# Binary cross-entropy on one core: the second half's negation moved behind the next chunk's clips

## The chip, the core and the metric

The kernel runs on one core of a Trainium2 chip. The metric is the device time of one execution in microseconds (us), as the median of several runs; lower is better. The engines that matter here are VectorE (DVE in the profile), ScalarE (ACT), GpSimd (POOL), whose instruction queue issues nearly all DMAs, and the core's 16 DMA engines, which move data between the chip's memory (HBM) and the on-chip buffer (SBUF).

## What is computed

```python
pred   = uniform(0.01, 0.99, (8192, 8192))  # float32
target = randint(0, 2, (8192, 8192))        # float32, 0 or 1
def reference(pred, target):
    eps = 1e-7
    pred = np.clip(pred, eps, 1 - eps)
    return -(target * np.log(pred) + (1 - target) * np.log(1 - pred))
```

Each of the three arrays holds 67,108,864 float32 values (268 MB). Since target is 0 or 1, one of the two terms is always zero, and the kernel uses that: the result is -log(|pred + target - 1|).

## The kernel before

The arrays are taken as one flat row of values and cut into chunks. A chunk is 128 partitions by some width: first one of 8192 columns (chunk 0), then 35 of 14336 columns (chunks 1 to 35; the name `z` is 35), then a tail of 6656, 6656 and 1024 columns (chunks 36 to 38, named a, b, c). Two buffers stay in SBUF. `ring_p` holds three wide chunks of pred in float32; a chunk is worked on in place there and stored from there. `ring_t` has room for one wide chunk of target, which the load turns into bfloat16 on the way.

The work on a chunk, in two halves of its columns (`halves`), is:

- `clip` (line 85, VectorE, tensor_scalar with max and min) bounds pred;
- `merge` (line 91, VectorE, scalar_tensor_tensor) makes pred + (target - 1); ScalarE then takes the absolute value (line 94) and the logarithm (line 95);
- `negate` (line 99, VectorE, tensor_scalar times -1) gives the result.

The DMAs of a wide chunk are `load_p` (line 70, pred), `load_t` (line 73, target) and `store` (line 79). All three are issued from GpSimd's queue (only chunk 0's pred comes through ScalarE's queue, and the tail's stores through SyncE's).

The order is written out by hand (`tc.manual_schedule()`): each engine takes its instructions in the order in which the program names them, and waits at an instruction until what it needs is there. One turn of the loop over k (lines 110 to 120) gives VectorE two merges of chunk k, the two negations of chunk k, and the two clips of chunk k+1. It gives ScalarE absolute value and logarithm of each half of chunk k. It gives GpSimd's queue the load of target k+1 (which waits for both merges, since `ring_t` holds one chunk only), the store of chunk k (which waits for the second negation) and the load of pred k+2 (which overwrites the slot of chunk k-1). Lines 121 to 141 finish chunk 35 and the tail.

Of the kernel before, what the change touches and what calls it, by code (L numbers as in the profile page):

```python
# [1 line left out]

# [4 lines left out]

EPS = 1e-7

WIDE = 14336  # L10
SLOTS = 3
TAIL = (6656, 6656, 1024)
ROWS = (108, 12, 8)


@with_exitstack
def kernel(
    ctx: ExitStack,
    tc: tile.TileContext,
    pred: bass.AP,  # L20
    target: bass.AP,
    out: bass.AP,
):
    nc = tc.nc
    fp32 = mybir.dt.float32
    low = mybir.dt.bfloat16
    Alu = mybir.AluOpType
    Act = mybir.ActivationFunctionType
    P = nc.NUM_PARTITIONS

    R, C = pred.shape
    total = R * C // P
    rest = total - sum(TAIL)
    n = rest // WIDE
    first = rest - n * WIDE
    assert 0 < first <= WIDE and n > 4 and sum(TAIL) <= WIDE
    spots = [(first, 0)]
    spots += [(WIDE, k % SLOTS * WIDE) for k in range(1, n + 1)]
    c = (n + 1) % SLOTS * WIDE
    for w in TAIL:  # L40
        spots.append((w, c))
        c += w
    n = len(spots)
    z = n - 1 - len(TAIL)
    starts = [sum(w for w, _ in spots[:k]) * P for k in range(n)]

    pool = ctx.enter_context(tc.tile_pool(name="rings", bufs=1))
    ring_p = pool.tile([P, SLOTS * WIDE], fp32, name="ring_p", tag="ring_p")
    ring_t = pool.tile([P, WIDE], low, name="ring_t", tag="ring_t")
    warm = pool.tile([1, 8], fp32, name="warm", tag="warm")  # L50

    def chunk(ap, k):
        flat = ap.rearrange("r c -> (r c)")
        w = spots[k][0]
        return flat[starts[k] : starts[k] + w * P].rearrange("(p w) -> p w", p=P)

    def cols(ring, k, part, c):
        w = spots[k][0]
        i, m = part
        return ring[:, c + i * w // m : c + (i + 1) * w // m]  # L60

    def p_of(k, part=(0, 1)):
        return cols(ring_p, k, part, spots[k][1])

    def t_of(k, part=(0, 1)):
        return cols(ring_t, k, part, spots[k][1] % WIDE)

    def load_p(k):
        queue = nc.scalar if k == 0 else nc.gpsimd
        queue.dma_start(out=p_of(k), in_=chunk(pred, k))  # L70

    def load_t(k):
        nc.gpsimd.dma_start(out=t_of(k), in_=chunk(target, k))  # L73

    def store(k):
        queue = nc.sync if k > z else nc.gpsimd
        r = 0
        for rows in ROWS if k == n - 1 else (P,):
            queue.dma_start(out=chunk(out, k)[r : r + rows, :], in_=p_of(k)[r : r + rows, :])  # L79
            r += rows  # L80
        assert r == P

    def clip(k, *part):
        p = p_of(k, *part)
        nc.vector.tensor_scalar(  # L85
            out=p, in0=p, scalar1=EPS, scalar2=1 - EPS, op0=Alu.max, op1=Alu.min
        )

    def merge(k, *part):
        p, t = p_of(k, *part), t_of(k, *part)  # L90
        nc.vector.scalar_tensor_tensor(  # L91
            out=p, in0=t, scalar=1.0, in1=p, op0=Alu.subtract, op1=Alu.add
        )
        nc.scalar.activation(out=p, in_=p, func=Act.Abs)  # L94
        nc.scalar.activation(out=p, in_=p, func=Act.Ln)  # L95

    def negate(k, *part):
        p = p_of(k, *part)
        nc.vector.tensor_scalar(out=p, in0=p, scalar1=-1.0, scalar2=None, op0=Alu.mult)  # L99

    halves = (0, 2), (1, 2)
    with tc.manual_schedule():
        load_p(0)
        load_t(0)
        load_p(1)
        nc.vector.memset(warm, 1.0)  # L106
        nc.scalar.activation(out=warm, in_=warm, func=Act.Ln)  # L107
        for h in halves:
            clip(0, h)
        for k in range(z):  # L110
            for h in halves:
                merge(k, h)
            load_t(k + 1)
            for h in halves:
                negate(k, h)
            for h in halves:
                clip(k + 1, h)
            store(k)
            if k + 2 <= z:
                load_p(k + 2)  # L120
        for h in halves:
            merge(z, h)
        a, b, c = range(z + 1, n)
        for j in a, b, c:
            load_p(j)
            load_t(j)
        negate(z, halves[0])
        clip(a)
        negate(z, halves[1])
        store(z)  # L130
        merge(a)
        clip(b)
        merge(b)
        negate(a)
        store(a)
        clip(c)
        merge(c)
        negate(b)
        store(b)
        negate(c)  # L140
        store(c)


# [1 line left out]
_INS = ['pred', 'target']  # L145
_OUTS = [((8192, 8192), 'float32')]


# [23 lines left out]
```

## Time and profile before

| what | value |
|---|---|
| median of three runs | 1867.55 us (1865.96 to 1867.95) |
| the profiled execution itself | 1868.84 us |
| its span, first to last instruction | 1867.1 us |
| VectorE busy | 1118.2 us, 60% of the span |
| ScalarE busy | 901.7 us, 48% |
| GpSimd busy | 283.3 us, 15% |
| moved by the 16 DMA engines | 671.14 MB, mean 359 GB/s |
| HBM read and written | 536.87 MB and 268.44 MB, 431 GB/s over the span |
| one merge of 128x7168 | about 7.6 us |
| one clip or negation of 128x7168 | about 3.9 us |
| one absolute value or logarithm of 128x7168 | about 6.2 us |

The profile is of one execution. Busy shares are averages over the span. In a line of the timeline, the first number is the start in microseconds from the span's beginning, the second the busy time, then come engine, source line, operation, output and input; the brackets say how long the engine sat idle before it and what released it. In a table by windows the last two columns are the mean busy share of the 16 DMA engines and the rate that they moved. The rate counts target once it is bfloat16, so the load of target shows half the rate of the other transfers at the same speed of reading. A "time to landing" runs from the issue of a DMA to the moment at which all of its data are there, the time that it stands in line behind others included.

### The profile page before, as it was taken

What the parts mean: (1) busy time and instruction counts of PE and PEld (TensorE: products, weight loads), DVE (VectorE), ACT (ScalarE), POOL (GpSimd) and SP (SyncE); (2) the same over time, 40 slices, a digit from 0 to 9 for tenths busy, and PEclk for the clock granted to TensorE, in tenths of its full rate; (3) what the DMA queues carried; (4) which work ended last, traced back from release to release, by engine and by line L of the source; (5) the groups of instructions that cost most, each with busy time, mean ns of one, the idle gap of its engine ahead of it and who ended that gap; (6) DMA issues with size and microseconds to landing.
All of it is one profiled execution on the core that took longest, in us unless ns stands there. A gap on an engine that the chain in (4) does not pass through costs nothing.

```text
span 1867.1 us, 695 instructions
## 1 busy us (share of the span) xinstructions
DVE 1118.2 (60%) x226; ACT 901.7 (48%) x152; POOL 283.3 (15%) x117
## 2 busy tenths in 40 slices
DVE  4675665655556555665665556655566665556664
ACT  3555444444555555444444555555544444455555
POOL 0121111111111101111111111101111111111100
DMA  9999999999999999999999999999999999999998
GB/s 331 336 373 373 364 355 359 356 355 355 354 354 359 373 373 373 370 356 362 356 354 358 354 354 356 367 373 373 373 362 360 359 354 359 354 354 354 360 366 346
DMA packets 16869, 671.14 MB, mean 359 GB/s; under 512 B 1888, under 2 KB 1888, under 8 KB 2272
## 3 DMA queue, kind: packets, MB, share of 16 engines
q0 software_dynamic: 16272, 659.56, 98.5%
q1 hardware_dynamic: 448, 7.34, 0.9%
q10 hardware_dynamic: 144, 4.19, 0.6%
q14 instruction: 5, 0.04, 0.0%
HBM read 536.87 MB, written 268.44 MB: 431 GB/s over the span
## 4 chain that ended last, share of the span: by engine, by line
DMA 67%; issue 28%; DVE 2%; ACT 2%; POOL 0%; POOLq 0%; DVEq 0%; PEldq 0%
DMA ring_t<-in_target_dram 67%; DVE ring_p L91 2%; ACT ring_p L95 1%; ACT ring_p L94 1%; DVE ring_p L99 0%; POOL out_dram L79 0%; POOL ring_p L70 0%; DVEq L167 0%; POOLq L73 0%; POOLq L79 0%; DVEq L91 0%; PEldq L167 0%
## 5 line engine op out<-in xcount | busy, mean ns | idle before, releaser
L94 ACT ACTIVATE ring_p<-ring_p 128x7168 f32<-128x7168 f32 (+3 forms) x75 | 451.6, 6021 | 943.5 <-DVE ring_p L91 943.5
L91 DVE SCALAR_TENSOR_TENSOR ring_p<-ring_t,ring_p 128x7168 f32<-128x7168 bf16 (+3 forms) x75 | 554.8, 7436 | 236.9 <-DMA ring_t<-in_target_dram 236.8
L99 DVE TENSOR_SCALAR ring_p<-ring_p 128x7168 f32<-128x7168 f32 (+3 forms) x75 | 285.0, 3801 | 475.0 <-ACT ring_p L95 475.0
L95 ACT ACTIVATE ring_p<-ring_p 128x7168 f32<-128x7168 f32 (+3 forms) x75 | 452.1, 6028 | 2.4
L85 DVE TENSOR_SCALAR ring_p<-ring_p 128x7168 f32<-128x7168 f32 (+3 forms) x75 | 281.8, 3798 | 20.1 <-DMA ring_p<-in_pred_dram 20.1
L79 POOL DMA_DIRECT2D out_dram<-ring_p x36 | 127.4, 3540 | 730.3 <-DVE ring_p L99 730.3
L73 POOL DMA_DIRECT2D ring_t<-in_target_dram x39 | 20.7, 532 | 802.9 <-DVE ring_p L91 802.1
L70 POOL DMA_DIRECT2D ring_p<-in_pred_dram x38 | 135.3, 3560 | 0.0
L107 ACT ACT_TABLE_LOAD x1 | 1.3, 1283 | 1.1 <-PEq L156 1.1
L106 DVE MEMSET warm<- 1x8 f32 x1 | 0.1, 65 | 0.8 <-PEq L156 0.8
L107 ACT ACTIVATE warm<-warm 1x8 f32<-1x8 f32 x1 | 0.2, 208 | 0.0
L156 POOL MEMSET const-float32-0.0<- 128x1 f32 x1 | 0.1, 98 | 0.2 <-issue 0.2
L156 POOL MEMSET const-bfloat16-1.0<- 128x1 bf16 x1 | 0.1, 101 | 0.0
L156 POOL MEMSET const-float32-1.0<- 128x1 f32 x1 | 0.1, 98 | 0.0
L156 POOL MEMSET const-uint8-127<- 128x1 uint8 x1 | 0.1, 98 | 0.0
## 6 DMA issues: line engine op xcount, KB each, us to landing
ring_p<-in_pred_dram POOLq DMA_DIRECT2D x35, 7168.0 KB, 44.3
out_dram<-ring_p POOLq DMA_DIRECT2D x35, 7168.0 KB, 31.0
ring_t<-in_target_dram POOLq DMA_DIRECT2D x35, 3584.0 KB, 35.2
ring_p<-in_pred_dram POOLq DMA_DIRECT2D x2, 3328.0 KB, 33.6
out_dram<-ring_p SPq DMA_DIRECT2D x2, 3328.0 KB, 15.1
ring_p<-in_pred_dram ACTq DMA_DIRECT2D x1, 4096.0 KB, 19.5
out_dram<-ring_p POOLq DMA_DIRECT2D x1, 4096.0 KB, 21.4
ring_t<-in_target_dram POOLq DMA_DIRECT2D x2, 1664.0 KB, 28.8
```

The source lines that it names most:

```text
L70: queue.dma_start(out=p_of(k), in_=chunk(pred, k))
L73: nc.gpsimd.dma_start(out=t_of(k), in_=chunk(target, k))
L79: queue.dma_start(out=chunk(out, k)[r : r + rows, :], in_=p_of(k)[r : r + rows, :])
L85: nc.vector.tensor_scalar(out=p, in0=p, scalar1=EPS, scalar2=1 - EPS, op0=Alu.max, op1=Alu.min)
L91: nc.vector.scalar_tensor_tensor(out=p, in0=t, scalar=1.0, in1=p, op0=Alu.subtract, op1=Alu.add)
L94: nc.scalar.activation(out=p, in_=p, func=Act.Abs)
L95: nc.scalar.activation(out=p, in_=p, func=Act.Ln)
L99: nc.vector.tensor_scalar(out=p, in0=p, scalar1=-1.0, scalar2=None, op0=Alu.mult)
L106: nc.vector.memset(warm, 1.0)
L107: nc.scalar.activation(out=warm, in_=warm, func=Act.Ln)
L156: nc = _bacc.Bacc("TRN2", target_bir_lowering=False, num_devices=1)
```

## The change

From the third chunk on (k of 2 and more, 33 of the 35 turns of the loop) VectorE's order within a turn is: negate the first half of chunk k, clip both halves of chunk k+1, negate the second half of chunk k. Before, both negations stood ahead of the clips. For k of 0 and 1 the order stays. The store of chunk k and the load of pred k+2 are named behind the last negation, as before. No instruction is added or taken away.

```diff
             for h in halves:
                 merge(k, h)
             load_t(k + 1)
-            for h in halves:
-                negate(k, h)
+            negate(k, halves[0])
+            if k < 2:
+                negate(k, halves[1])
             for h in halves:
                 clip(k + 1, h)
+            if k >= 2:
+                negate(k, halves[1])
             store(k)
             if k + 2 <= z:
                 load_p(k + 2)
```

## The prediction

> **What bounds the kernel now.** I first read the page's row of DMA shares and its queue table.
>
> ```profile
> DMA  9999999999999999999999999999999999999998
> q0 software_dynamic: 16272, 659.56, 98.5%
> q1 hardware_dynamic: 448, 7.34, 0.9%
> q10 hardware_dynamic: 144, 4.19, 0.6%
> ```
>
> The shares of the three queues add up to 100% of 16 engines' span: the DMA engines are hardly ever without a packet, while VectorE is busy for 60% and ScalarE for 48%. Next, the chain that ended last; one turn of its steady pattern is
>
> ```profile
> 713.58 15.49 issue
> ...
> 729.08 35.17 DMA ring_t<-in_target_dram
> ```
>
> Taken alone this looks like a loop: target lands, VectorE merges for 15.2 us, the next target load is issued, and it takes 35.2 us. But those 35.2 us are not a target transfer. The table by windows cuts that turn (713.60 to 764.34 us, 50.74 us long) into thirds:
>
> ```profile
> 713.60:730.51 16.91, 15.16 (x2) 9.19 (x2) 0.53 (x1) 1.00 1.00 434
> 730.51:747.42 16.91, 5.33 (x2) 15.41 (x3) 0.00 (x0) 1.00 1.00 373
> 747.42:764.34 16.92, 10.07 (x3) 0.00 (x0) 7.44 (x2) 1.00 1.01 278
> ```
>
> The last two columns are DMA share and GB/s. The share is 1.00 in each third. A turn moves three equal portions (store, pred, target) of 128x14336 values, in the order of their issue, each in a third, 16.9 us. The target load, issued at 729.08, stands behind what is left of store and pred for some 18 us. So the turn is 3 x 16.9 = 50.7 us of transfer, and the merges hide beside it. The kernel is bound by DMA, and an edit counts only if it leaves DMA engines empty or saves a transfer. This one saves none.
>
> **The change, step by step.** It adds and removes no instruction. In 33 turns it moves one negation (3.89 us) behind two clips (3.81 us from start to start, 7.70 us for the pair). What hangs on it is the order of events in a turn, shown by the timeline:
>
> ```profile
> 729.08 0.53 POOL L73 DMA_DIRECT2D ring_t<-in_target_dram  x1 [22.18 <-DVE ring_p L91]
> 733.71 3.89 DVE L99 TENSOR_SCALAR ring_p<-ring_p 128x7168 f32<-128x7168 f32 x1 [4.92 <-ACT ring_p L95]
> 745.98 3.89 DVE L99 TENSOR_SCALAR ring_p<-ring_p 128x7168 f32<-128x7168 f32 x1 [8.38 <-ACT ring_p L95]
> 749.79 7.70 DVE L85 TENSOR_SCALAR ring_p<-ring_p 128x7168 f32<-128x7168 f32 x2
> 750.17 3.63 POOL L79 DMA_DIRECT2D out_dram<-ring_p  x1 [20.55 <-DVE ring_p L99]
> 753.79 3.82 POOL L70 DMA_DIRECT2D ring_p<-in_pred_dram  x1
> 764.35 15.16 DVE L91 SCALAR_TENSOR_TENSOR ring_p<-ring_t,ring_p 128x7168 f32<-128x7168 bf16 x2 [6.86 <-DMA ring_t<-in_target_dram]
> ```
>
> 1. The gap that the clips would fill. VectorE idles 8.38 us, from 737.60 to 745.98, for ScalarE's second logarithm. The clips need the next pred chunk, issued at 703.09 in the turn before; the look at that one line says when it is there:
>
> ```profile
> L70 POOL DMA_DIRECT2D ring_p<-in_pred_dram x1: 3820/3820/3820, 703.1 to 703.1; - x1
> ...
> DMA to landing us min/median/max: 44.3/44.3/44.3
> ```
>
> 703.1 + 44.3 = 747.4 us. So the clips can't start at 737.6; VectorE now waits there about 9.8 us for pred, past the end of the logarithm at 745.95.
>
> 2. The negation behind them. Clips from 747.4 to 755.1, the negation to 759.0. Queued behind the waiting clips on VectorE are this negation and then the next merges. The merges wait for target, which lands at 764.26, so VectorE still has 5.3 us to spare (it had 6.86 idle, as the clips ended at 757.5). The next turn's merges, target load and logarithms keep their times: cost nothing, hidden by the target transfer; if pred landed 5.3 us later relative to target, it would start to cost.
>
> 3. The store and the pred load behind it on GpSimd's queue. The store is released 0.30 us after the negation's end (749.87 to 750.17 before), so at 759.3 instead of 750.2: 9.1 us later. Beside the clips the two issues took 3.63 and 3.82 us; without VectorE beside it an issue takes 0.53 (the target's line above). VectorE is now idle there, so store and pred are issued by 759.8 and 760.4, against 753.8 and 757.6: only 6.0 and 2.8 us later. The Trainium skill states this for the issues, in "SBUF — State Buffer", section "SBUF: two separate sides": while VectorE runs a fast-mode operation on SBUF, GpSimd can't write DMA descriptors and DMA engines may starve. The trace agrees on 3.63 against 0.53 us; by that rule alone some starvation would end and the kernel gain, by the DMA share of 1.00 none was there to end.
>
> 4. Is 759.8 soon enough? The store follows target on the DMA engines:
>
> ```profile
> 755.88:757.99 2.11, 1.61 (x1) 0.00 (x0) 1.73 (x1) 1.00 1.01 217
> 757.99:760.11 2.12, 0.00 (x0) 0.00 (x0) 0.00 (x0) 1.00 1.01 325
> 760.11:762.22 2.11, 0.00 (x0) 0.00 (x0) 0.00 (x0) 1.00 1.01 380
> 762.22:764.34 2.12, 0.00 (x0) 0.00 (x0) 0.00 (x0) 1.00 1.00 433
> ```
>
> At 217 GB/s all engines carry target, at 433 all carry the store. The hand-over is spread: by the trace's records of single packets (8 per engine and transfer, 2.1 us each) the first engine is through with target at 759.8, the last at 763.9. What is not in the trace is the time from a GpSimd issue to the first packet when the engines have nothing else queued. Nearest rows: pred of chunk 0, issued from ScalarE's queue at 0.73, has its first packet at 1.74, so 1.0 us; the tail's store from SyncE's queue follows its negation (end 1850.4) at 1851.3, 0.9 us. Above, target of chunk 0, issued by GpSimd at 1.23, has its first packet at 6.05, 4.8 us, but behind pred's packets. I take 1.0, as nearest: an idle queue. Then the store can start at 759.3 + 1.0 = 760.3 (760.8 counted from the end of the issue). Engines through at 759.8 wait up to 1 us, once; the last, at 763.9, waits for nothing, with 3.1 to 3.6 us to spare. As target lands only when the last engine is done, the turn stays 50.74 us. Engines that had run ahead are held back, and lose a lead that never counted. With the low end (0 us) nothing waits at all. With 4.8 us the store starts at 764.1, the last engine waits about 0.15 us per turn, 33 x 0.15 = 5 us. The Trainium skill, in "DMA: Bandwidth & Descriptors", section "Latency and other measured facts", gives about 1 us to the first byte for DMAs issued by GpSimd, more than for the other queues; no row here isolates it, and by it the sum would be the same.
>
> 5. The ends. Turns 0 and 1 are as before. In turn 34 the store goes from 1765.5 to about 1774.6, and pred of chunk a just behind it, while target of chunk 35 is in transfer until 1779; the tail isn't touched.
>
> **Sum:** 0 us on the profiled execution's 1868.84 us (span 1867.1 plus 1.7 around it). That run lies 1.3 us above the median of 1867.55, so I give 1867.6 for the median.
>
> **Rivals.**
>
> *The DMA engines fall into step* (slower). The early turns are longer than the late ones: in the chain, target issues lie 51.2 to 51.4 us apart between 168 and 323 us, mostly 50.7 after 470. In the packet records the last target packet of some engines, ahead of the store, takes up to 0.76 us longer while the engines are close in step (ends 0.6 to 3 us apart) and almost never once they are 4.2 us apart. The change holds back the leaders to about 3 us ahead of the last engine. If the engines stay close in step and the last one pays 0.5 us in each of 33 turns, that is 16.5 us, less the 4 us or so that before pays anyway: +12, 1880 us. It decides from the point at which the held-back engines lengthen the last engine's packets, not just their own. Against it: the last engine hands over 3 us after the bunch, alone, and with such a spread the turn from 322 to 373 us took 50.8 us. Chance 0.13.
>
> *The store's first packet comes late* (slower). If it takes more than 4.6 us from issue, every turn waits: at 4.8 us 1872; each further 0.1 us costs 3.3 us. No row asks for more. Chance 0.06.
>
> *The lengthened packets vanish* (faster). At the hand-over at 100 us, where the store was issued only 6 us ahead (94.14), no packet was lengthened, though engines were 0.5 us apart; in others it had been issued 10 us ahead. If a late store spares them, the last engine wins back the 4 us or so by which it falls behind the first: 1863.5, just over 0.2%. Chance 0.06, as it has one hand-over for it.
>
> *The change reaches its gap, but it doesn't matter*: were pred there at 737.6, the store would keep its time, and again nothing would change. It belongs to the forecast's time.
>
> **How the numbers follow.** Forecast, no change: 0.75. The bound for "same" is 0.2%, 3.7 us, about what a measurement of this kernel can tell from no change. Slower: 0.13 + 0.06 = 0.19; faster 0.06; same 0.75. The range goes from 1863 (the rival below) to 1878: it holds the 4.8 us bound (1872) and most of the way to 1880.
>
> **What would show it.** Right: clips (line 85) wait about 9.8 us per turn for pred, some 320 us in all; the second negation waits for nothing; store issues take 0.53 us; time to landing falls from 31.0 to about 22 us for the store (781.2 - 759.3) and from 44.3 to about 38 for pred; turns stay 50.7 us; DMA share 1.00. Wrong: turns above 51 us past 500 us; a DMA share under 0.98 where target ends; target landing before its merges can start, which would put VectorE on the path.

## The result, and the profile after

The changed kernel takes 1880.94 us (median of 4 runs, 1879.8 to 1881.97) against 1866.88 us for the kernel before, measured anew beside it: a ratio of 1.0075, 95% interval 1.0058 to 1.0092. The forecast of no change was wrong, and the range, up to 1878, missed it by 3 us. The profiled execution took 1879.8 us with a span of 1878.0, 10.9 us more than before.

Nearly everything that the prediction said about VectorE and GpSimd is in the profile. From the groups of instructions (line, engine, operation, forms, count, busy us, mean ns, idle us before them and its releaser):

```profile
L85 DVE TENSOR_SCALAR ring_p<-ring_p 128x7168 f32<-128x7168 f32 (+3 forms) x75 | 281.8, 3797 | 344.7 <-DMA ring_p<-in_pred_dram 344.7
...
L99 DVE TENSOR_SCALAR ring_p<-ring_p 128x7168 f32<-128x7168 f32 (+3 forms) x75 | 284.7, 3798 | 198.4 <-ACT ring_p L95 198.4
L79 POOL DMA_DIRECT2D out_dram<-ring_p x36 | 25.5, 708 | 1029.1 <-DVE ring_p L99 1029.1
```

The clips now wait 344.7 us for pred (20.1 before), the negations 198.4 us for the logarithm (475.0 before), and a store issue takes 0.7 us on average (3.5 before). From the table of DMA issues (KB each, median us to landing):

```profile
ring_p<-in_pred_dram POOLq DMA_DIRECT2D x35, 7168.0 KB, 38.7
out_dram<-ring_p POOLq DMA_DIRECT2D x35, 7168.0 KB, 22.3
ring_t<-in_target_dram POOLq DMA_DIRECT2D x35, 3584.0 KB, 35.5
```

The prediction gave about 38 for pred and 22 for the store. The one surprise is target: 35.5 us, where the same table of the kernel before has 35.2. The chain that ended last shows the same as turns, from one target issue to the next. First the kernel before, then the changed one:

```profile
1084.23 35.14 DMA ring_t<-in_target_dram
...
1134.92 35.18 DMA ring_t<-in_target_dram
...
1185.65 35.20 DMA ring_t<-in_target_dram
...
1236.40 35.19 DMA ring_t<-in_target_dram
```

```profile
1087.85 35.31 DMA ring_t<-in_target_dram
...
1138.70 36.23 DMA ring_t<-in_target_dram
...
1190.48 35.42 DMA ring_t<-in_target_dram
...
1241.45 36.16 DMA ring_t<-in_target_dram
```

The turns of the changed kernel are 50.85, 51.78 and 50.97 us long, where before they were 50.69, 50.73 and 50.75. The row of DMA shares and the queue table do not show where that goes:

```profile
DMA  9999999999999999999999999999999999999998
...
q0 software_dynamic: 16272, 659.56, 98.6%
```

The engines count as busy as ever, and the bytes are the same. What fell is the rate, from 359 to 357 GB/s over the whole span. The table by windows of 380 and 400 us (last columns DMA share, GB/s), first of the kernel before, then of the changed one:

```profile
120.00:500.00 380.00, 225.49 (x46) 185.82 (x31) 59.23 (x22) 1.00 1.00 359
900.00:1300.00 400.00, 242.69 (x48) 192.76 (x32) 63.71 (x24) 1.00 1.00 363
```

```profile
120.00:500.00 380.00, 225.97 (x46) 185.76 (x31) 11.07 (x21) 1.00 1.00 359
900.00:1300.00 400.00, 242.74 (x48) 186.78 (x31) 12.66 (x24) 1.00 1.00 357
```

In the first 500 us the two are alike; later the changed kernel moves 357 GB/s instead of 363 at the same share. The size of that step is not to be relied on, since a window cuts turns in two and target counts half: from 1300 to 1700 us the kernel before shows 360 as well. But the turns are longer, and packets in them take longer. One such place, in windows of 2.1 us at the end of a store:

```profile
1131.80:1133.90 2.10, 2.10 (x1) 2.10 (x1) 0.00 (x0) 1.00 1.01 437
1133.90:1136.00 2.10, 2.10 (x1) 2.10 (x1) 0.00 (x0) 1.00 1.33 437
1136.00:1138.10 2.10, 2.10 (x1) 2.07 (x2) 0.00 (x0) 1.00 1.01 437
```

A packet is counted in the window in which it starts, with its whole length. A share of 1.33 says that the packets which start there last a third longer than the others. The trace's records of single packets (8 per engine and transfer, usually 2.12 us each) name no engine; the packets of one engine are found by joining the end of each to the start of the next. By them, these are the last packets of the store: 13 of the 16 engines take 0.7 to 1.1 us longer for them. The other three run over elsewhere, at the end of target. In the next turn, for example, target's last packet takes them 3.15 to 3.24 us instead of 2.13, starting at 1170.3 to 1171.5 us, while the 13 begin the store.

From the store of chunk 1 to that of chunk 34, each of the 13 engines runs over by 9.5 to 11.4 us in all at the store's last packet and by at most 1.1 us at target's last two. With the three it is the other way round: 13.1 to 14.0 us at target's last two packets, at most 0.4 us at the store's last. From turn 14 on it is always these three that are through with target last. Target has landed only when the last engine is through with it, so it is their part that lengthens the turns. In the three turns above the last engine's target packets run over by 0.14, 1.19 and 0.18 us. Over the whole stretch the packets of the engine that is last in most turns run over by 14.7 us, and those of the last engine before by 4.4 us (3.0 at target's end, nearly all in turns 2 to 7). The difference is 10.3 of the 10.9 us by which the span grew.

### The profile page after: what moved, and what is told of

It reads as the page before. It is cut to its first block, busy times and chain, and to the rows that moved or that the text cites. A ratio compares the mean times of both kernels' runs of the same rounds, so it can differ in the third digit from the quotient of the medians.

```text
span 1878.0 us, 695 instructions
## 1 busy us (share of the span) xinstructions
DVE 1117.9 (60%) x226; ACT 901.7 (48%) x152; POOL 72.7 (4%) x117
## 4 chain that ended last, share of the span: by engine, by line
DMA 67%; issue 28%; DVE 2%; ACT 2%; POOL 0%; POOLq 0%; DVEq 0%; PEldq 0%
DMA ring_t<-in_target_dram 67%; DVE ring_p L91 2%; ACT ring_p L95 1%; ACT ring_p L94 1%; DVE ring_p L99 0%; POOL out_dram L79 0%; POOL ring_p L70 0%; DVEq L170 0%; POOLq L73 0%; POOLq L79 0%; DVEq L91 0%; PEldq L170 0%
## 5 line engine op out<-in xcount | busy, mean ns | idle before, releaser
L85 DVE TENSOR_SCALAR ring_p<-ring_p 128x7168 f32<-128x7168 f32 (+3 forms) x75 | 281.8, 3797 | 344.7 <-DMA ring_p<-in_pred_dram 344.7
L99 DVE TENSOR_SCALAR ring_p<-ring_p 128x7168 f32<-128x7168 f32 (+3 forms) x75 | 284.7, 3798 | 198.4 <-ACT ring_p L95 198.4
L79 POOL DMA_DIRECT2D out_dram<-ring_p x36 | 25.5, 708 | 1029.1 <-DVE ring_p L99 1029.1
L70 POOL DMA_DIRECT2D ring_p<-in_pred_dram x38 | 26.6, 701 | 0.0
## 6 DMA issues: line engine op xcount, KB each, us to landing
ring_t<-in_target_dram POOLq DMA_DIRECT2D x35, 3584.0 KB, 35.5
```

The source lines that it names most:

```text
L85: nc.vector.tensor_scalar(out=p, in0=p, scalar1=EPS, scalar2=1 - EPS, op0=Alu.max, op1=Alu.min)
```

## The experiments

In all of them the reference time is that of the kernel before on the same chip, 1867.0 to 1867.6 us. Times are medians; ratios and intervals are worked out over the runs of both kernels, and can differ a little from the ratio of the medians. The diffs are cut to the lines that matter, and `# k >= 2` stands for the condition on the turn. **Lead** means here: from the end of the issue of a store (or of pred) to the moment at which the first DMA engine is through with the transfer ahead of it, by the packet records. In the kernel before, the store's lead is 5.3 to 9.4 us, in the changed one 3.7 us at first and 0.3 to 1.5 us from turn 10 on.

### What of the change costs: clips early, store late, or pred late

First kernel, only the store (and pred behind it) late:

```diff
+            negate(k, halves[0])
+            negate_cols(k, WIDE // 2, WIDE - 64)   # k >= 2
             for h in halves:
                 clip(k + 1, h)
+            negate_cols(k, WIDE - 64, WIDE)        # k >= 2
             store(k)
```

> VectorE keeps the order of before, except that the last 64 of the 14336 columns of a chunk are negated behind the two clips, from the third chunk on. So clips and negations lie where they lay, and only the issues of store and next pred come later, at about 6 us ahead of the merges instead of 14 us (5 us in the changed kernel), and no longer beside a clip. Theory 'late issue' (the DMA engines lengthen packets at their hand-overs because store and pred are queued late): 1876 to 1881 us, turns of about 51.1 us. Rival 'clips' (the clips' earlier place beside the target transfer disturbs it): 1867 us, turns of 50.7 us.

Measured: 1878.99 us, ratio 1.0064 (1.0043 to 1.0085). The clips lie where they lay, and most of the loss is there, 11.4 of 14 us.

Second kernel, only the pred load late:

```diff
             store(k)
             if k + 2 <= z:
+                if k >= 2:
+                    nc.vector.memset(p_of(k + 2)[:, 0:8], 0.5)
                 load_p(k + 2)
```

> Order of before; a write of 8 columns into the slot of the next-but-one pred chunk stands behind the clips, so that the pred load is issued about 4 us later (some 6 us ahead of the merges), while the store keeps its place, 14 us ahead. If the late pred load alone causes the loss: 1876 to 1881 us. If it is the late store, or the clips: 1867 us.

Measured: 1868.89 us, ratio 1.0003 (0.9993 to 1.0013). Its timeline has the store in its old place, and the issue of pred starts 4 us later than before:

```profile
1106.91 3.62 POOL L79 DMA_DIRECT2D out_dram<-ring_p  x1 [20.55 <-DVE ring_p L99]
1114.17 0.07 DVE L121 MEMSET ring_p<- 128x8 f32 x1
1114.54 0.53 POOL L70 DMA_DIRECT2D ring_p<-in_pred_dram  x1 [4.01 <-DVE ring_p L121]
1120.66 7.62 DVE L91 SCALAR_TENSOR_TENSOR ring_p<-ring_t,ring_p 128x7168 f32<-128x7168 bf16 x1 [6.42 <-DMA ring_t<-in_target_dram]
```

Behind the clips that issue takes 0.53 us, and not 3.82 as before beside them. So it ends 5.6 us ahead of the merges, where it was 6.7 before and 4.2 in the changed kernel: a part of pred's lateness only. The run below with pred released behind the first merge answers for the rest.

Third kernel, the negation behind one clip:

```diff
+            negate(k, halves[0])
+            clip(k + 1, halves[0])
+            negate(k, halves[1])                   # k >= 2
+            clip(k + 1, halves[1])
             store(k)
```

> From the third chunk on the second negation stands behind one clip only, the other clip follows it. The store is released about 3.8 us sooner than in the changed kernel, some 9 us ahead of the merges, and its issue lies beside the second clip again; pred follows at some 5 us ahead. Theory 'late issue': between the two, 1868 to 1875 us. If what counts is that issues lie beside no clip, or that store and pred are issued back to back: 1867 us. If the clips' earlier place counts: about 1874 us or more.

Measured: 1880.69 us, ratio 1.0067 (1.0047 to 1.0087): all of the loss, where I had expected a part. The store's issue starts 10 us ahead of the merges, but lies beside the second clip and takes 3.6 us, so its lead was 0 to 1.6 us from turn 8 on. So far it is the late store that costs, or that store and pred are issued within a microsecond of each other.

### Each turn, or a pattern that the early turns set

These two are cut against the changed kernel. First, its order up to turn 17 only:

```diff
-            if k < 2:            # and k >= 2 below
+            if not 2 <= k < 18:  # and 2 <= k < 18 below
```

> The changed order in turns 2 to 17 only, then the order of before. If each turn in the changed order costs by itself: about half the loss, 1872 to 1875 us, with turns of 50.7 us soon after turn 18. If the early turns set a pattern of the DMA engines that then stays (what the engines' phases are by turn 18 decides): 1879 us or more, with turns of 51 us to the end.

Measured: 1873.61 us, ratio 1.0028 (1.0017 to 1.0038), 6 of the 14 us. And the other way round, the changed order from turn 18 on:

```diff
-            if k < 2:            # and k >= 2 below
+            if k < 18:           # and k >= 18 below
```

> The changed order from turn 18 on only, by when the kernel before runs at 50.7 us per turn with the DMA engines up to 4.2 us apart. If each turn in the changed order costs by itself: half the loss, 1873 to 1875 us, with turns near 51.1 us from 18 on. If the phases that the engines have reached keep the hand-overs undisturbed whatever the order: 1867 us, turns of 50.7 us to the end.

Measured: 1877.11 us, ratio 1.0052 (1.0037 to 1.0067). Its chain shows the loss set in behind the first late store, that of turn 18, issued at 962.1:

```profile
881.27 35.13 DMA ring_t<-in_target_dram
...
931.96 35.18 DMA ring_t<-in_target_dram
...
982.69 35.51 DMA ring_t<-in_target_dram
...
1033.75 35.87 DMA ring_t<-in_target_dram
```

The turns are 50.69, 50.73 and 51.06 us long, and the next is 51.41. The engines were 3 us apart by then (first engine through with target at 963.7, last at 966.8). So the cost is that of each late store, whatever the phases before. This half came out at 9.7 us, somewhat above half of the loss.

### Late, or back to back with pred

Early and back to back, by a side operation that keeps the clips away from the issues:

```diff
+            if k >= 2:
+                nc.vector.scalar_tensor_tensor(  # 1500 columns of scratch
+                    out=fill, in0=fill, scalar=1.0, in1=fill, op0=Alu.mult, op1=Alu.max)
             for h in halves:
                 clip(k + 1, h)
             store(k)
```

> Order of before; from the third chunk on VectorE does a side operation of about 1.6 us on a scratch buffer between the second negation and the clips. So store and next pred are issued back to back, 0.5 us each, beside no clip, some 14 us ahead of the merges; the clips end 1.6 us later, still ahead of target. Theory 'late store' (it counts how long ahead of its hand-over the store is queued): 1867 us. Rival 'back to back' (it counts that store and pred are queued within 1 us of each other, as in all three slow kernels so far, and not 4 us apart as in before): 1876 to 1881 us, with the store's last packets lengthened.

Measured: 1867.14 us, ratio 0.9999 (0.9989 to 1.0008). The two issues stand 0.5 us apart, and nothing is lost; the store's last packet kept its length in every turn:

```profile
1104.70 0.54 POOL L80 DMA_DIRECT2D out_dram<-ring_p  x1 [20.55 <-DVE ring_p L100]
1105.23 0.53 POOL L71 DMA_DIRECT2D ring_p<-in_pred_dram  x1
1105.95 7.69 DVE L86 TENSOR_SCALAR ring_p<-ring_p 128x7168 f32<-128x7168 f32 x2
```

Late and apart, in the changed order, with two side operations and a write of 8 columns between `store(k)` and `load_p(k + 2)`:

> Order of the changed kernel, but the pred load waits for two side operations on VectorE and a write of 8 columns into its slot, so that it follows the store by about 4 us, some 1 us ahead of the merges; the store is as late as in the changed kernel. Theory 'late store': 1878 to 1883 us. Rival 'back to back': 1867 us, the store's last packets at their usual 2.1 us.

Measured: 1882.13 us, ratio 1.0075 (1.0058 to 1.0091). Back to back is out, a late store it is.

### How late is too late

One clip ahead of the negation, and the second clip held back, so that the issues are short:

```diff
+            clip(k + 1, halves[0])
+            negate(k, halves[1])   # k >= 2
+            side()                 # 1500 columns of scratch, 1.7 us
+            clip(k + 1, halves[1])
             store(k)
```

> Like the kernel with the negation behind one clip, but a side operation of 1.6 us holds the second clip back, so that store and pred are issued back to back beside no clip, each in 0.5 us: store ready about 4 us ahead of the first DMA engine's end of target, where the slow kernels had 0 to 2 us. Theory 'lead' (a store queued less than about one packet, 2.1 us, ahead of the hand-over has its last packets lengthened; with more it has not): 1867 to 1869 us, store packets at 2.1 us. If being behind any clip, or back to back with pred, were enough: 1876 to 1881 us.

Measured: 1867.12 us, ratio 1.0002 (0.9993 to 1.0012). The same with one and a half clips ahead:

> The same with the negation behind one and a half clips and the side operation behind it: store ready about 2 us ahead of the first engine's end of target. Theory 'lead' with its border near 2.1 us: between the two, 1868 to 1874 us, with the store's last packets lengthened only in turns in which the lead is under about 2 us. If there is no such border but a cost that grows all along: about 1873 us with packets lengthened in all turns.

Measured: 1878.01 us, ratio 1.0058 (1.0043 to 1.0073), above what I had expected. The timelines of the two, first with one clip, then with one and a half:

```profile
1110.51 0.54 POOL L80 DMA_DIRECT2D out_dram<-ring_p  x1 [25.78 <-DVE ring_p L100]
1111.03 0.53 POOL L71 DMA_DIRECT2D ring_p<-in_pred_dram  x1
...
1119.49 15.16 DVE L92 SCALAR_TENSOR_TENSOR ring_p<-ring_t,ring_p 128x7168 f32<-128x7168 bf16 x2 [3.85 <-DMA ring_t<-in_target_dram]
```

```profile
1114.61 0.54 POOL L80 DMA_DIRECT2D out_dram<-ring_p  x1 [27.67 <-DVE ring_p L100]
1115.14 0.53 POOL L71 DMA_DIRECT2D ring_p<-in_pred_dram  x1
...
1122.65 7.62 DVE L92 SCALAR_TENSOR_TENSOR ring_p<-ring_t,ring_p 128x7168 f32<-128x7168 bf16 x1 [4.76 <-DMA ring_t<-in_target_dram]
```

The store is issued 9.0 us ahead of the merges in the one and 8.0 us in the other, and this one microsecond is worth 10.9 us of the whole. By the packet records the first engine is through with target at 1114.75 and 1116.68, so the leads are 3.7 and 1.5 us. With one and a half clips the turns up to 15 have 2.1 us or more of lead and no long store packet; the engines drift apart, the first ends earlier, and from turn 16 on the lead is under 2 us. Taken over turns 2 to 34 of twelve kernels (the two of the change, the nine experiments above, and the one in the next section), 396 turns in all:

| store's lead, us | turns | mean overrun of the store's last packet, us per engine | mean overrun of target's last two packets, us, at the last engine |
|---|---|---|---|
| under 1 | 65 | 0.46 | 0.25 |
| 1 to 1.5 | 75 | 0.23 | 0.71 |
| 1.5 to 2 | 17 | 0.06 | 0.50 |
| 2 to 2.5 | 11 | 0.01 | 0.19 |
| 2.5 to 14 | 228 | 0.00, at most 0.01 | 0.19 (0.08 from turn 12 on) |

The store's packets follow each engine's own lead, from the end of the issue to the moment at which that engine is through with target. With under 1 us of its own, an engine's last store packet was over 0.1 us too long in all 443 cases (0.72 us in the mean), with 1 to 1.5 us in 854 of 882, with 1.5 to 2 us in 275 of 493, with 2 to 2.5 us in 12 of 188, with more in 2 of 4330. And within the 140 turns whose lead is under 1.5 us, the engines with 2.5 us or more of their own (508 cases) have no long store packet, but run over by 0.49 us in the mean at target's end, which those with under 2 us never do by more than 0.14 us.

### Clips early without a late store

ScalarE negates the second half, behind its logarithm:

```diff
+                p = p_of(k, halves[1])             # k >= 2
+                nc.scalar.activation(out=p, in_=p, func=Act.Copy, scale=-1.0)
             for h in halves:
                 clip(k + 1, h)
             store(k)
```

> From the third chunk on ScalarE negates the second half, right behind its logarithm, in about 6.2 us; VectorE's clips come as soon as pred is there, as in the changed kernel, and the store is released some 12 us ahead of the merges, ready at the clips' end, about 9 us ahead. Theory 'lead': 1867 to 1869 us, since the store is ready over 4 us ahead of its hand-over though the clips lie as early as in the changed kernel. Rival 'clips early': 1876 to 1881 us.

Measured: 1868.05 us, ratio 1.0001 (0.9992 to 1.0011). The clips lie as early as in the changed kernel and cost nothing; the store's lead is 3.3 us in the median turn. (It falls to 1.0 us in the last turns, and there the store's last packets do run over, by up to 0.3 us.) The kernel is no faster than before either: VectorE's freed time is not on the path.

### Only the store, or any transfer in line

The store in two DMAs, the first half released early:

```diff
-            store(k)
+            for h in halves:       # k >= 2
+                store_half(k, h)   # one DMA of 7168 columns each
```

> Order of the changed kernel, but from the third chunk on the store is two DMAs, one for each half: the first half is queued behind the first negation, some 26 us ahead of the merges, the second half where the whole store was, some 5 us ahead, back to back with pred. Theory 'late store': the hand-over from target finds the first half queued long before, and the second half is needed 8 us later, so 1867 us, or up to 1870 for the smaller packets. Rival 'back to back': 1876 to 1881 us.

Measured: 1874.92 us, ratio 1.0034 (1.0021 to 1.0047), between the two and above what I had expected. The store's packets, now 1.06 us each, no longer run over, and no transfer has a short lead: the first half is issued 13 us or more ahead, and the second half's lead over the end of the first is 2.1 us or more. Yet target's last packets run over, by 4.0 us in all (mean over the engines, 0.9 before). So a short lead is not all that lengthens target's end. The issues of the second half and of pred fall here among the hand-overs from target, from 2.9 us ahead of the first to 6 us and more behind it. Whether an issue at that moment costs by itself is not separated by any run; in the kernel with only pred late, pred's issue falls there too in the later turns, and no loss shows.

Pred at the last moment, released by VectorE between the merges (its load at the old place stays for k of 0 and 1):

```diff
+            merge(k, halves[0])
+            if 3 <= k < z:
+                side(); side()     # 1400 columns of scratch each, 3.3 us
+                nc.vector.memset(p_of(k + 1)[:, 0:8], 0.5)
+                load_p(k + 1)
+            merge(k, halves[1])
             load_t(k + 1)
```

> Order and store of before; from turn 3 on the next pred chunk is loaded late instead, released by VectorE between the two merges, ready about 1 us ahead of the first DMA engine's end of the store. If a short lead costs whichever transfer it is: pred's last packets lengthened, 1874 to 1885 us. If it is peculiar to the store: 1867 to 1869 us.

Measured: 1894.27 us, ratio 1.0151 (1.0131 to 1.0172), more than expected. Pred's lead over the store's end is 3.1 to 4.0 us up to turn 7, and 0.7 to 2.1 us from turn 8 on. Pred's last packets, which I had expected to run over, keep their length. Its first packets run over by 5.6 us in all, and above all target behind it does: 16.7 us at its last packet and 2.9 at the one before (means over engines), against 0.9 before. The same without the side operations:

> Like the kernel that loads pred at the last moment, but without the two side operations: pred is released right behind the first merge, ready about 4 us ahead of the first DMA engine's end of the store instead of 0 to 2 us. Theory 'lead' (the border of about 2 us holds for pred as for the store): 1867 to 1869 us. If any pred load behind the store's start costs: 1875 us or more.

Measured: 1867.9 us, ratio 1.0005 (0.9996 to 1.0015), with leads of 3.3 to 7.4 us. So for pred, too, 3.3 us are enough, and 0.7 to 2.1 are not. It also answers for pred's part in the change: pred is issued here with far less lead than in the changed kernel (17.8 us in the turn at 1118 us), and nothing is lost.

The stores from another queue, in the changed order:

```diff
-        queue = nc.sync if k > z else nc.gpsimd
+        queue = nc.sync if k >= 2 else nc.gpsimd
```

> Order of the changed kernel, but the stores from the third chunk on are issued from SyncE's queue instead of GpSimd's; the issue is as late as in the changed kernel. If the short lead costs only in GpSimd's queue (how its transfers are queued one behind the other): 1867 to 1871 us, no lengthened packets at the store's end. If it costs on the DMA engines whatever the queue: 1876 us or more. It may also go above that, because packets of two queues then alternate and pred no longer stands behind the store.

Measured: 1911.03 us, runs from 1894 to 1952, ratio 1.0207 (1.016 to 1.0255) without the longest. This is so much, and so uneven, that it tells nothing of the lead. The profile, of the run of 1952 us, shows that the line of store, pred and target is gone: the load of pred now waits for a store of the other queue to land.

```profile
1101.45 3.32 POOL L70 DMA_DIRECT2D ring_p<-in_pred_dram  x1 [18.28 <-DMA out_dram<-ring_p]
```

## Why the prediction was wrong, point by point

- **The bound** was right: DMA, 50.7 us of transfer per turn, and VectorE's work beside it. ScalarE's negating and the freed issues of GpSimd moved nothing.
- **Steps 1 to 3** were right to a few tenths. In the turn at 1106 us the changed timeline reads

```profile
1106.16 7.70 DVE L85 TENSOR_SCALAR ring_p<-ring_p 128x7168 f32<-128x7168 f32 x2 [9.80 <-DMA ring_p<-in_pred_dram]
1113.77 3.88 DVE L99 TENSOR_SCALAR ring_p<-ring_p 128x7168 f32<-128x7168 f32 x1
1117.95 0.54 POOL L79 DMA_DIRECT2D out_dram<-ring_p  x1 [29.58 <-DVE ring_p L99]
1118.48 0.53 POOL L70 DMA_DIRECT2D ring_p<-in_pred_dram  x1
1123.25 15.16 DVE L91 SCALAR_TENSOR_TENSOR ring_p<-ring_t,ring_p 128x7168 f32<-128x7168 bf16 x2 [5.59 <-DMA ring_t<-in_target_dram]
```

  with a wait of 9.80 us (9.8 forecast), the store 5.3 us ahead of the merges (5.0), an issue of 0.54 us (0.53), and merges that still wait for target (5.59 us, 5.3 forecast).
- **Step 4 failed**: "Engines through at 759.8 wait up to 1 us, once; the last, at 763.9, waits for nothing, with 3.1 to 3.6 us to spare." It priced the store's lateness by when its first packet can start, and by the wait for it. That part was right: in the turn at 1118 us the store's first packet starts 1.10 us after its issue did (1117.95 to 1119.05), and the last engine never waits for the store. But the runs showed that a start in time is not enough. An engine that is through with target less than about 2 us, one packet's length, after the store's issue ends has a longer last store packet, a full transfer later (0.72 us with under 1 us, 0.40 with 1 to 1.5). And the engines still on target, for which the step had time to spare, take longer for target's last packets: the last one 14.0 us in all, 3.0 before, and this is what lengthens the turns. The price of 0 to 5 us, from bounds of 0 to 4.8 us for the first packet, left this out, as it knew no cost except waiting.
- In the same step, the Trainium skill's "DMA: Bandwidth & Descriptors", section "Latency and other measured facts", gives about 1 us to the first byte for DMAs issued by GpSimd. The trace agrees, with the 1.10 us above. But as the time by which a store must be queued ahead it is too short: with 1 to 1.5 us of lead the store's last packets run over by 0.23 us per engine, with 2.5 us by nothing.
- **The rival "The DMA engines fall into step"** gave 1880 us, the time that was measured, and it had the place on the path: target's last packets at the last engine, 0.5 us a turn by the rival, 0.45 by the trace (14.5 us in turns 2 to 33). The engines are held back to 3.3 to 4.1 us apart from turn 12 on, about as it said. What it had wrong is the condition. In the first kernel of the experiments the engines are 4.2 to 4.9 us apart from turn 13 on, and it loses 11.4 us; with one clip ahead and short issues they are 3.8 to 4.6 us apart from turn 10 on, and it loses nothing. What tells them apart here is the store's lead, at most 1.4 us in those turns of the one and over 3.3 us in the other. The turn from 322 to 373 us, named against the rival, had a lead of 7 us, and so could not speak for a late store. The long store packets of the other engines are not in it at all. Its number was thus in part luck, but the chance of 0.13 was too low for what it had right.
- **The rival "The store's first packet comes late"** looked at the right distance, from the store's issue to a hand-over, but asked for a first packet over 4.6 us after the issue; it came after 1.10 us.
- **"The lengthened packets vanish"** rested on one hand-over, at 100 us, with a lead of 2.4 us. The kernels with a long lead keep the early turns' lengthened target packets: 0.9 us (mean over engines) with the early back-to-back issue, 0.9 before. What lengthens those is a different matter, and not settled here.
- **What would show it:** the sign "turns above 51 us past 500 us" came true; "DMA share 1.00" came true as well, and proved nothing, since an engine in a long packet counts as busy.

**What stays open.** That a late store costs is shown by the runs above, turn by turn. Why it does is not: why a short lead shows in an engine's last store packet, a full transfer further on, and why the engines still on target are held up at the same hand-over. The half stores show that target's end can run over without any short lead. Nor is it shown whether the border belongs to GpSimd's queue or to the DMA engines: the run from SyncE's queue changed too much else.

## What to carry to other kernels

In a kernel bound by a line of DMAs, an issue is not free as long as it comes "before the last engine needs it": look at the first engine's hand-over, and keep a packet and a half (here 3 us) between the end of an issue and that moment, as the kernels here that lost nothing did. Moving work behind other work on a compute engine that is idle a lot can still cost, by what its last instruction releases. A DMA share of 1.00 tells that engines hold packets, not that they move bytes: compare the length of turns, or single packets.

## What the hardware showed beyond that

- The loss grows over the run: in the changed kernel the store's last packets keep their length up to turn 10 (at most 0.02 us over), while the 16 DMA engines drift from 0.5 to 2.7 us apart and the lead falls from 3.6 to 1.5 us.
- A store's issue by GpSimd beside two clips took 3.6 us against 0.54 us without them; the early back-to-back issue thus freed some 6 us of GpSimd's time per turn and gained nothing (ratio 0.9999).
- One microsecond in the store's issue (9.0 or 8.0 us ahead of the merges) separates 1867.12 from 1878.01 us.
